# A decoder step on one core: late value pages also on ScalarE, key pages also on GpSimd, more slack for TensorE's small work, transfers issued by free buffer, and row scaling folded into a product

## The chip, the cores and the metric

One core of a Trainium2 chip. The time is the device time of one execution in microseconds, the median of several; the kernel before took 1545.37 us (three runs, 1544.26 to 1545.92). Engines are called PE (TensorE), DVE (VectorE), ACT (ScalarE), POOL (GpSimd) and SP (the queue that issues every DMA).

## The reference, cut to what matters

One layer of a hybrid decoder for 512 prompt tokens and 8 single-token samples, all in float32, model width 2048.

- Rows are normalised (`u = rms_norm(x, g_norm)`) and multiplied by `w_in` (2048 x 7168) into queries, keys, values, two gates and the input of a convolution. The prompt runs differential attention (two softmax maps per head, eight heads) and a 31-tap depthwise convolution with layer norm; both halves go through `w_out` (2048 x 2048), then `h += sigmoid(rmsnorm(h) W_pg) * (p W_ple)` and a last RMSNorm.
- The eight samples do the same for one token each, but attend to a paged cache of 4096 past keys and values: 8 x 32 pages of 128 positions, 512 KB per key page and per value page, found through `page_table`. For a sample, `score = q . k` for 16 maps per position, softmax over all positions, `a = p0 - lam * p1` per head, and `o[h] = sum over positions of a[pos, h] * v[pos, h, :]`.

So 256 key pages and 256 value pages (268 MB) are read beside some 70 MB of weights.

## The kernel before, in words

**Main products.** The weights come in slots of 256 x 512 (512 KB, tile `raw`, three buffers). Each half slot is split into a rounded part `hi` (ACT) and a rest `lo` (POOL, sometimes DVE), three buffers of each; the activations stand split as `aht` and `alt`. A half slot is 12 PE products into the four `acc` banks: hi x aht, hi x alt, lo x aht for four token tiles. The slots run in a fixed order: k, q, v, the convolution's inputs, the gates, `w_out`, `w_pw`, and in the end `w_ple` and `w_pg` with two half passes for the last columns.

**Everything else is small work laid between them.** The program is laid out at build time by a planner (class `Planner`, L61): it keeps an estimated clock for each engine (`clk`) and an estimated ready time for each tile (`plan.ready`). After every three main products `hook` (L354) runs: it issues weights and pages (`wpump`, `kring.pump`, `vring.pump`: SP), splits weights ahead, advances waiting tasks (generators with conditions made by `on`, L276), and calls `decode_tick` (L562). Each engine then runs its list in order, so a wrong estimate shows as a wait in the trace. PE's small work may only be placed at each fourth hook (`turn`, `TURNS`), that is after 12 main products, and `on("PE", ...)` asks that what it reads is ready 500 ns before PE's clock.

**Pages.** Key pages come through the ring `kt` (5 buffers), value pages through `vt` (2 buffers), and through `kt` too when no key is left to issue. A buffer is refilled when its reader is planned to end within 500 ns; the three sources are asked in a fixed order (weights, `kt`, `vt`). A key page is multiplied by the broadcast query `qb` on DVE (one 128x1024 TENSOR_TENSOR) and summed in groups of 64 by DVE (TENSOR_REDUCE) or, when DVE is planned over 400 ns late and no other such page is under way, by 16 ACT activations with an accumulator. When the 32 pages of a sample are summed, `softmax` makes `aw`. A value page is four PE products `pers<-vt,aw`, side by side in four column groups (two records each in the trace); `v_pages` (L607) takes all pages planned ready, one at the least at a group's last hook and two otherwise. `v_end` (L518) picks the heads out of `pers` when a sample's 32 pages are done. After the eighth, `sample_tail` (L1406) runs the samples through `w_out` and `w_pg` by "tail pages" through the same two rings.

**The start.** Four row tiles are loaded into `ct`, `dt` and two halves of `ft`. `rows_stat` makes the norm factor of each row, `rows_scale` (DVE) scales the first 512 columns, `rows_rest` (POOL, 12 calls) the other 1536, and PE transposes 128x128 blocks against the identity (`rows_T` for the first three column blocks, `u_T` for the other 13), four per block; `u_split` makes `aht` and `alt` from the transposed block. Two of the POOL calls stand before the fourth tile's statistics and ten stand after the second slot half's start, ahead of the `lo` splits that follow on POOL's list.

All instructions but a few are recorded under line 216 (the helper that emits them), so groups are told apart by tile names.

Of the kernel before, what the change touches and what calls it, by code (L numbers as in the profile page):

```python
# [221 lines left out]
def hymba_step(ctx, tc, x_prompt, x_sample, p_prompt, p_sample, cache_k, cache_v, state_conv, page_table,  # L222
# [123 lines left out]
    step = [0]  # L346

# [6 lines left out]
    def hook(n=7):  # L354
        step[0] = n
        wpump()
        kring.pump()
        vring.pump()
        if cur[0] < 168:
            split_ahead()  # L360
        for t in list(tasks):
            for _ in range(3):
# [33 lines left out]
    class Ring:  # L396
# [15 lines left out]
        def pump(self):  # L412
            while self.n < self.used + self.size and (self.n < self.size or self.freed[0] <= clk["PE"] + 500):
                kind = self.next_kind()
                if kind is None:
                    return
# [12 lines left out]
                self.n += 1  # L429

# [87 lines left out]
    def v_end(s):  # L518
# [7 lines left out]
        if vper[0] == s:  # L526
# [18 lines left out]
            yield from gather(ps)  # L545
        ended[0] += 1
# [6 lines left out]
    K_LATE = 400  # L553
# [8 lines left out]
    def decode_tick(at):  # L562
        if not dec["on"]:
            return
        now = clk["PE"]
        while True:
            more = k_next()
            pend = dec["pend"]
            if pend and (len(pend) > 1 or not more):
                s, pg, kt = pend[0]  # L570
                if k_act_live[0] < 1 and clk["A"] <= now + 300 and clk["V"] > now + K_LATE and plan.ready(kt) <= now + 800:
                    pend.pop(0)
                    k_act_live[0] += 1
                    spawn(k_act(s, pg, kt), rank=2)
                elif clk["V"] <= now + 400:
                    pend.pop(0)
                    V.tensor_reduce(out=dec["sc"][s][:, pg, :], in_=kt.rearrange("p (x d) -> p x d", d=64), axis=AX.X, op=ADD)
                    k_did(s, kt)
                else:
                    break  # L580
            elif more and clk["V"] <= now + 400:
                s, pg = divmod(dec["ik"], NPAGE)
                if pg == 0:
                    dec["sc"][s] = scp.tile([128, NPAGE, 16], F32, tag="sc", name="sc")
                kt, _ = kring.get()
                V.tensor_tensor(out=kt, in0=kt, in1=qbt[s], op=MUL)
                pend.append((s, pg, kt))
                dec["ik"] += 1
                if pg == NPAGE - 1 and s + 1 < NSEQ:
                    spawn(prep_qb(s + 1), rank=0)  # L590
            else:
                break
        v_pages(at == 7)

    def v_here():
# [9 lines left out]
        return n  # L605

# [1132 lines left out]
```

## Time and profile before

| | before |
|---|---|
| median of the runs | 1545.37 us |
| profiled execution | 1543.31 us, span 1541.5 us |
| PE busy | 1464.2 us, 95% of the span |
| DVE, ACT, POOL busy | 1089.7, 852.6, 627.3 us |
| DMA | 424.4 MB, mean 275 GB/s |

The span runs from the first to the last instruction; 1.8 us of the profiled execution lie outside it. PE's records overlap their neighbours (a product of 512 columns is recorded with some 0.4 us and the next begins 0.23 us later), so steps are read from starts and from the chain, not from the durations. A fp32 product leaves two records.

### The profile page before, as it was taken

The numbers are of one execution on the slowest core, as the hardware profiler recorded it, in microseconds if no ns is written. First come the engines' busy times: TensorE is split into PE (matmuls) and PEld (weight loads), VectorE is DVE, ScalarE is ACT, GpSimd is POOL, SyncE is SP. The second block draws the span as 40 slices with busy tenths as digits, with TensorE's granted clock in tenths as the row PEclk, the third lists the DMA queues.
The fourth block names the chain that finished last, engine by engine and source line by source line (L and its number), as shares of the span: only waits on it lengthen the run. The fifth ranks groups of instructions, "written<-read, shape, count | busy, mean of one in ns | idle before, by whom it ended". The sixth has DMA issues, their size and how long they took to land.

```text
span 1541.5 us, 32434 instructions
## 1 busy us (share of the span) xinstructions
PE 1464.2 (95%) x10448; PEld 1037.8 (67%) x10448; DVE 1089.7 (71%) x1625; ACT 852.6 (55%) x4162; POOL 627.3 (41%) x471
## 2 busy tenths in 40 slices
PE   5999999999999999999999999999999999999986
PEld 4677877766767666667767666677767776666653
DVE  5278888887998888888879789777787695110212
ACT  4256775666537566664456775656655675131332
POOL 5144534333433333333433445244333355343642
PEclk8999999999999999999999999999999999999998
DMA  8758779776877777674488848799887798999778
GB/s 292 270 175 289 268 259 372 275 283 232 283 260 236 256 264 247 219 247 151 153 307 281 301 155 296 259 355 349 304 325 261 252 379 315 351 328 346 268 265 283
DMA packets 148923, 424.42 MB, mean 275 GB/s; under 512 B 14192, under 2 KB 16226, under 8 KB 148480
## 3 DMA queue, kind: packets, MB, share of 16 engines
q1 hardware_dynamic: 148752, 422.35, 77.6%
q8 instruction: 82, 1.34, 0.4%
q14 instruction: 89, 0.73, 0.1%
HBM read 413.62 MB, written 9.63 MB: 275 GB/s over the span
## 4 chain that ended last, share of the span: by engine, by line
PE 73%; DMA 12%; DVE 6%; POOL 3%; ACT 2%; issue 2%; SPq 1%; POOLq 0%; ACTq 0%; DVEq 0%
PE acc L216 55%; PE pers L216 11%; PE misc L216 6%; DMA raw<-in_w_in_dram 4%; POOL lo L216 3%; DMA vt<-in_cache_v_dram 3%; DVE kt L216 2%; DMA raw<-in_w_out_dram 1%; DMA kt<-in_cache_k_dram 1%; DMA kt<-in_w_pg_dram 1%; SPq L216 1%; DVE sc L216 1%; ACT hi L216 1%; DVE bt L216 1%; DMA raw<-in_w_pg_dram 1%
## 5 line engine op out<-in xcount | busy, mean ns | idle before, releaser
L216 POOL TENSOR_TENSOR lo<-raw,hi 128x512 fp32r<-128x512 f32 x392 | 560.7, 1442 | 808.0 <-ACT hi L216 783.1
L216 ACT CAST hi<-raw 128x512 fp32r<-128x512 f32 x392 | 237.0, 617 | 431.4 <-PE acc L216 230.0
L216 ACT ACTIVATE kt<-kt 128x64 f32<-128x64 f32 x1568 | 378.5, 244 | 18.0 <-DVE kt L216 18.0
L216 PE MATMUL acc<-hi,aht 128*128 128x512 f32 x896 | 374.2, 418 | 7.8 <-ACT hi L216 7.6
L216 DVE TENSOR_TENSOR kt<-kt,qb 128x1024 f32<-128x1024 f32 x256 | 352.8, 1391 | 38.7 <-DMA kt<-in_cache_k_dram 35.3
L216 PE MATMUL acc<-lo,aht 128*128 128x512 f32 x896 | 359.9, 402 | 14.4 <-POOL lo L216 14.3
L216 PE MATMUL acc<-hi,alt 128*128 128x512 f32 x896 | 356.4, 398 | 0.2 <-DVE alt L216 0.2
L216 ACT ACTIVATION_READ_ACCUMULATOR kt<-kt 128x1 f32 x1568 | 296.3, 189 | 0.0
L216 PE MATMUL acc<-aht,hi 128*128 128x512 f32 x576 | 242.4, 421 | 4.2 <-ACT aht L216 3.4
L216 PE MATMUL acc<-aht,lo 128*128 128x512 f32 x576 | 229.6, 399 | 2.1 <-POOL lo L216 2.0
L216 PEld LDWEIGHTS acc<-hi,aht 128*128 128x128 f32 x896 | 169.7, 189 | 87.0 <-ACT hi L216 25.9
L216 PE MATMUL acc<-alt,hi 128*128 128x512 f32 x576 | 228.3, 396 | 0.0
L216 PEld LDWEIGHTS acc<-lo,aht 128*128 128x128 f32 x896 | 169.7, 189 | 65.8 <-POOL lo L216 26.1
L216 PEld LDWEIGHTS acc<-hi,alt 128*128 128x128 f32 x896 | 170.3, 190 | 34.4 <-DVE alt L216 0.8
L216 DVE TENSOR_REDUCE sc<-kt 128x16 f32<-128x1024 f32 x158 | 189.8, 1209 | 1.3
L216 DVE SCALAR_TENSOR_TENSOR misc<-ft,wdwT,misc 128x512 f32<-128x512 f32 x240 | 180.0, 750 | 6.3
L216 PEld LDWEIGHTS acc<-aht,hi 128*128 128x128 f32 x576 | 108.8, 189 | 64.3 <-issue 32.1
L216 PEld LDWEIGHTS acc<-aht,lo 128*128 128x128 f32 x576 | 108.7, 189 | 31.7 <-POOL lo L216 5.8
L216 PE MATMUL pers<-vt,aw 128*8 128x256 f32 x1656 | 114.1, 380 | 13.9 <-DVE pers L216 9.4
L216 PEld LDWEIGHTS acc<-alt,hi 128*128 128x128 f32 x576 | 108.9, 189 | 21.0 <-DVE alt L216 0.4
L216 DVE SCALAR_TENSOR_TENSOR acc<-acc,ct 128x512 f32<-128x512 f32 x16 | 11.2, 700 | 128.2 <-ACT acc L216 128.1
L216 PEld LDWEIGHTS pers<-vt,aw 128*8 128x8 f32 x1656 | 33.9, 88 | 67.5 <-issue 24.9
(259 smaller groups left out, 1273.2 us busy)
## 6 DMA issues: line engine op xcount, KB each, us to landing
kt<-in_cache_k_dram SPq DMA_DIRECT2D x256, 512.0 KB
vt<-in_cache_v_dram SPq DMA_DIRECT2D x207, 512.0 KB
raw<-in_w_in_dram SPq DMA_DIRECT2D x112, 512.0 KB
kt<-in_cache_v_dram SPq DMA_DIRECT2D x49, 512.0 KB
raw<-in_w_pg_dram SPq DMA_DIRECT2D x40, 512.0 KB
raw<-in_w_out_dram SPq DMA_DIRECT2D x32, 512.0 KB
kt<-in_w_in_dram SPq DMA_DIRECT2D x12, 512.0 KB
kt<-in_w_out_dram SPq DMA_DIRECT2D x12, 512.0 KB
```

Source lines behind the costliest of these rows:

```text
L216: real(*args, **kw)
```

## The change

1. `on("PE", ...)` asks for 800 ns of slack instead of 500; value pages taken by PE must be ready 600 ns before PE's clock instead of 0.
2. Weights, `kt` and `vt` are issued by one function `pump`, the buffer that comes free first first, and 300 ns ahead instead of 500.
3. Late value pages by ACT. When the last key page of the last sample has been multiplied, the buffer of `qb` becomes an accumulator (`vacc`). From then on a value page may go to ACT: eight activations of 128x128, each scaled by its head's weight in `aw`, in place (or straight into `vacc` for the first page), two pages at a time; DVE then adds the page to `vacc` (128x1024). While that is possible PE takes value pages only when four are ready. At the sample's end eight small PE products sum `vacc` over the positions.
4. Key pages: POOL may do the multiplication when DVE's clock is over 700 ns ahead of PE's and POOL's at least 100 ns behind; ACT may sum two pages at a time, already when DVE's clock is ahead of PE's at all (before 400 ns); any ready page may be taken, not only the oldest.
5. The rows are not scaled any more: a 128x128 diagonal `xg` per row tile (identity times the norm factor, DVE, one `tmp` buffer until the last block) is the right operand of a plain fp32 product in place of the transpose against the identity. The 12 POOL calls are gone, and the DVE calls shrink from 512 to 128 columns.

```diff
+    PE_BACK, V_BACK = 800.0, 600.0
...
-        back = -500.0 if eng == "PE" else 500.0
+        back = -PE_BACK if eng == "PE" else 500.0
...
-        wpump()
-        kring.pump()
-        vring.pump()
+        pump()
...
+    PUMP = 300
+    def pump():
+        while True:
+            due = [(d, n, f) for n, (d, f) in enumerate(((wdue(), lambda: wpump(once=True)), (kring.due(), lambda: kring.pump(True)),
+                                                          (vring.due(), lambda: vring.pump(True)))) if d is not None]
+            if not due or min(due)[0] > clk["PE"] + PUMP:
+                return
+            min(due)[2]()
...
+        if s in vacc:
+            ps = yield from take("misc")
+            V.memset(ps[:, 0:256], 0.0)
+            yield on("PE", ps[:, 0:256], vacc[s])
+            for h in range(8):
+                a, g = h // 4, h % 4
+                mm(ps[32 * g:32 * g + 8, a * 128:(a + 1) * 128], cst[:, C_ROW + 7 - s:C_ROW + 15 - s],
+                   vacc[s][:, h * 128:(h + 1) * 128], start=False, stop=True, cost=7 if g else 205)
+            va_free.append(plan.ready(vacc.pop(s), True))
+            yield from gather(ps)
...
-    K_LATE = 400
+    K_LATE, K_POOL, K_LIVE = 0, -100, 2
...
-                if k_act_live[0] < 1 and clk["A"] <= now + 300 and clk["V"] > now + K_LATE and plan.ready(kt) <= now + 800:
+                if k_act_live[0] < K_LIVE and clk["A"] <= now + 300 and clk["V"] > now + K_LATE:
...
+            eng = V if clk["V"] <= now + 400 else G if clk["G"] <= now + K_POOL and clk["V"] > now + 700 and len(pend) < 3 else None
...
+            eng.tensor_tensor(out=kt, in0=kt, in1=qbt[s], op=MUL)
...
+            elif pg == NPAGE - 1:
+                va_free.append(plan.ready(qbt[s], True))
+        v_aside()
         v_pages(at == 7)
...
+    V_ACT, V_LIVE = 300, 2
+    def v_aside():
+        now = clk["PE"]
+        while v_pend and clk["V"] <= now + 500 and v_pend[0][0] in va_has and plan.ready(v_pend[0][1]) <= now + 600:
+            s, vt, ring = v_pend.pop(0)
+            V.tensor_tensor(out=vacc[s], in0=vacc[s], in1=vt, op=ADD)
...
+            if clk["A"] > now + V_ACT or v_act_live[0] >= V_LIVE:
+                return
...
+    def v_act(s, pg, vt, ring, out, first):
+        for h in range(8):
+            c = slice(h * 128, (h + 1) * 128)
+            yield lambda: clk["A"] <= clk["PE"] + 400
+            A.activation(out=out[:, c], in_=vt[:, c], func=AF.Copy, scale=aw[s % 2][:, pg, h:h + 1])
...
-                if kind != VALS or idx // NPAGE != s or plan.ready(t) > clk["PE"]:
+                if kind != VALS or idx // NPAGE != s or plan.ready(t) > clk["PE"] - V_BACK:
...
+    V_MANY = 4
...
-        if n < (1 if tiled else 2) or not turn():
+        if n < (V_MANY if s_aside() else 1 if tiled else 2) or not turn():
...
-                PE.transpose(ps[:, t * 128:(t + 1) * 128], xt[t][k // 4][:, (k % 4) * 128:(k % 4 + 1) * 128], ident)
+                mm(ps[:, t * 128:(t + 1) * 128], xt[t][k // 4][:, (k % 4) * 128:(k % 4 + 1) * 128], xg[:, t * 128:(t + 1) * 128])
...
-            V.tensor_scalar(out=xbig[t][:, 0, :], in0=xbig[t][:, 0, :], scalar1=stat[:, 8 + t:9 + t], scalar2=None, op0=MUL)
+            V.tensor_scalar(out=xg[:, t * 128:(t + 1) * 128], in0=ident, scalar1=stat[:, 8 + t:9 + t], scalar2=None, op0=MUL)
...
-        def rows_rest(t, n):
-            x = xbig[t][:, n, :]
-            G.tensor_tensor(out=x, in0=x, in1=stat[:, 8 + t:9 + t].to_broadcast([128, 512]), op=MUL)
...
-        rows_rest(0, 1)
-        rows_rest(1, 1)
...
-                for n in range(1, 4):
-                    for t in range(2 if n == 1 else 0, 4):
-                        rows_rest(t, n)
```

## Rows read from the trace of the kernel before

**Rows 1.** The page, parts 1 and 2: busy time of each engine, and PE's and the DMA engines' busy share over 40 slices of the span, in tenths.

```profile
PE 1464.2 (95%) x10448; PEld 1037.8 (67%) x10448; DVE 1089.7 (71%) x1625; ACT 852.6 (55%) x4162; POOL 627.3 (41%) x471
PE   5999999999999999999999999999999999999986
...
DMA  8758779776877777674488848799887798999778
```

**Rows 2.** Busy time of each engine by stretch: the stretch and its length in us, then PE, weight loads, DVE, ACT, POOL (with counts), PE's granted clock, the DMA share and GB/s.

```profile
240.00:700.00 460.00, 448.55 (x3166) 313.16 (x3165) 395.31 (x731) 286.67 (x1435) 172.75 (x141) 1.00 0.75 261
700.00:960.00 260.00, 255.77 (x1759) 183.83 (x1759) 220.35 (x273) 152.91 (x816) 111.53 (x76) 1.00 0.69 236
...
1295.00:1427.00 132.00, 131.34 (x965) 84.65 (x965) 20.82 (x39) 31.91 (x76) 47.36 (x38) 1.00 0.96 346
1427.00:1541.50 114.50, 89.62 (x1024) 58.02 (x1022) 25.03 (x52) 37.87 (x77) 49.57 (x44) 0.96 0.77 272
```

**Rows 3.** What PE waited for over the whole span: us in total, times, longest.

```profile
PE acc L216 <- POOL lo L216: 16.6, 25, 4.9
PE pers L216 <- DVE pers L216: 10.1, 13, 2.8
...
PE misc L216 <- ACT tmp L216: 7.4, 5, 3.9
...
PE pers L216 <- DMA vt<-in_cache_v_dram: 4.4, 7, 1.5
```

**Rows 4.** The start: one group of POOL's row scaling (busy us, mean ns of one), then rows of the timeline (start us, us), then two stretches with the columns of rows 2.

```profile
L216 POOL TENSOR_TENSOR ft<-ft,stat 128x512 f32<-128x512 f32 x6 | 6.3, 1068 | 0.0
...
24.18 1.04 POOL L216 TENSOR_TENSOR ct<-ct,stat 128x512 f32<-128x512 f32 x1
...
32.16 2.48 POOL L216 TENSOR_TENSOR lo<-raw,hi 128x512 fp32r<-128x512 f32 x2
...
33.47 0.61 PE L216 MATMUL acc<-lo,aht 128*128 128x512 f32 x1 [4.86 <-POOL lo L216]
...
33.40:36.60 3.20, 3.13 (x14) 2.99 (x15) 0.80 (x2) 1.38 (x2) 2.47 (x3) 0.55 0.84 252
...
38.30:41.00 2.70, 2.70 (x21) 2.39 (x19) 1.41 (x2) 2.08 (x4) 0.11 (x1) 1.00 0.10 31
```

**Rows 5.** The chain of work that ended last (start us, us, what, records): the transposes of the start at two clock levels, six main products, visits to two and three value pages, the 12 main products between visits, and four fp32 products of 128x128x128 (two records each).

```profile
34.08 2.56 PE misc L216 x12
...
38.32 1.31 PE misc L216 x12
39.63 1.40 PE acc L216 x6
...
1295.92 0.98 PE pers L216 x16
1296.90 3.01 PE acc L216 x12
...
1304.89 1.41 PE pers L216 x24
...
1367.00 0.89 PE misc L216 x8
```

**Rows 6.** The instructions that read or write `aw` (PE's are the value pages, eight records a page), by stretch: PE, weight loads, DVE.

```profile
1295.00:1427.00 132.00, 34.95 (x544) 11.85 (x544) 0.43 (x1) 1.00 0.96 346
```

**Rows 7.** The instructions that read or write `qb` by stretch: DVE (the key multiplications, one a page) and ACT.

```profile
60.00:240.00 180.00, 69.99 (x50) 2.15 (x4) 1.00 0.76 269
240.00:700.00 460.00, 104.54 (x78) 2.15 (x4) 1.00 0.75 261
960.00:1295.00 335.00, 121.70 (x89) 2.15 (x4) 0.98 0.85 307
```

**Rows 8.** Groups of the whole span (busy us, mean ns of one, idle before): the key multiplication and its sum on DVE, the sum by ACT, ACT's scaled copy of 128x128, and POOL's split.

```profile
L216 DVE TENSOR_TENSOR kt<-kt,qb 128x1024 f32<-128x1024 f32 x256 | 352.8, 1391 | 38.7 <-DMA kt<-in_cache_k_dram 35.3 <-ACT qb L216 2.6
L216 DVE TENSOR_REDUCE sc<-kt 128x16 f32<-128x1024 f32 x158 | 189.8, 1209 | 1.3
L216 ACT ACTIVATE kt<-kt 128x64 f32<-128x64 f32 x1568 | 378.5, 244 | 18.0 <-DVE kt L216 18.0
L216 ACT ACTIVATE bt<-misc,vec 128x128 f32<-128x128 f32 x32 | 11.4, 364 | 5.5 <-PE misc L216 5.3
L216 POOL TENSOR_TENSOR lo<-raw,hi 128x512 fp32r<-128x512 f32 x392 | 560.7, 1442 | 808.0 <-ACT hi L216 783.1 <-PE acc L216 12.4 <-PE misc L216 6.1
```

**Rows 9.** Timeline of POOL and DVE from 1270 to 1294 us (start us, us).

```profile
1289.38 1.28 POOL L216 TENSOR_TENSOR bt<-bt,tmp 128x512 f32<-128x512 f32 x1
1290.62 2.27 POOL L216 TENSOR_TENSOR lo<-raw,hi 128x512 fp32r<-128x512 f32 x1
...
1271.98 1.21 DVE L216 TENSOR_TENSOR kt<-kt,qb 128x1024 f32<-128x1024 f32 x1
...
1290.42 3.55 DVE L216 TENSOR_TENSOR kt<-kt,qb 128x1024 f32<-128x1024 f32 x2
```

**Rows 10.** One of PE's waits from 1440 us to the end (us in total, times, longest), and the last piece of the chain in which PE works (start us, us).

```profile
PE misc L216 <- DMA kt<-in_w_pg_dram: 2.8, 5, 0.9
...
1524.10 0.91 PE acc L216 x3
```

More of the change, by code (lines that the diff above doesn't have):

```diff
@@ L361, in hook @@
         for t in list(tasks):
-            for _ in range(3):
+            for _ in range(STEPS):
                 if t[0] is not None and not t[0]():
@@ L410, in next_kind, with due, pump @@
             return TAIL if left[TAIL] else None
-        def pump(self):
-            while self.n < self.used + self.size and (self.n < self.size or self.freed[0] <= clk["PE"] + 500):
+        def due(self):
+            if self.n >= self.used + self.size or self.next_kind() is None:
+                return None
+            return self.freed[0] if self.n >= self.size else 0.0
+        def pump(self, once=False):
+            while self.due() is not None and self.due() <= clk["PE"] + PUMP:
                 kind = self.next_kind()
-                if kind is None:
-                    return
                 idx = issued[kind]
@@ new lines, in decode_tick @@
+            pend.append((s, pg, kt))
+            dec["ik"] += 1
+            if pg == NPAGE - 1 and s + 1 < NSEQ:
+                spawn(prep_qb(s + 1), rank=0)
+            elif pg == NPAGE - 1:
+                va_free.append(plan.ready(qbt[s], True))
+        v_aside()
+        v_pages(at == 7)
+    va_free, vacc, va_has, v_act_live, v_pend = [], {}, set(), [0], []
+    V_ACT, V_LIVE = 300, 2
[4 more added lines that the diff above has]
+            V.tensor_tensor(out=vacc[s], in0=vacc[s], in1=vt, op=ADD)
+            ring.done(vt)
+            v_did(s)
+        while True:
+            ring = v_ring(600)
+            s, pg = divmod(dec["iv"], NPAGE)
+            if ring is None or not dec["soft"][s] or plan.ready(aw[s % 2]) > now + 500 or not (s in vacc or va_free) or len(v_pend) > 2:
+                return
+            if clk["A"] > now + V_ACT or v_act_live[0] >= V_LIVE:
+                return
+            first = s not in vacc
+            if first:
+                vacc[s] = plan.begin(qbp.tile([128, 1024], F32, tag="qb", name="qb"), va_free.pop(0))
+            vt, _ = ring.get()
+            dec["iv"] += 1
+            out = vacc[s] if first else vt
+            v_act_live[0] += 1
+            spawn(v_act(s, pg, vt, ring, out, first), rank=2)
@@ L595, in v_here, with v_did, v_ring @@
+    def v_did(s):
+        vdone[s] += 1
+        if vdone[s] == NPAGE:
+            spawn(v_end(s), rank=0)
+    def v_ring(ahead=0):
+        best = min((r for r in (kring, vring) if r.tiles and r.tiles[0][1] == VALS), key=lambda r: r.tiles[0][2], default=None)
+        return best if best and best.tiles[0][2] == dec["iv"] and plan.ready(best.tiles[0][0]) <= clk["PE"] + ahead else None
     def v_here():
@@ L614, in v_pages @@
         for k in range(n):
-            ring = kring if kring.here(VALS) and (not vring.here(VALS) or kring.tiles[0][2] < vring.tiles[0][2]) else vring
+            ring = v_ring(-V_BACK)
+            if ring is None:
+                break
             vt, idx = ring.get()
@@ L749, in hymba_step, with wdue, wpump @@
     raw_freed = []
-    def wpump(most=RAWB):
-        while (wst["issued"] < len(slots) and wst["issued"] < wst["released"] + most
-               and (wst["issued"] < RAWB or raw_freed[0] <= clk["PE"] + 500)):
+    def wdue():
+        if wst["issued"] >= min(len(slots), wst["released"] + RAWB):
+            return None
+        return raw_freed[0] if wst["issued"] >= RAWB else 0.0
+    def wpump(most=RAWB, once=False):
+        while wdue() is not None and wst["issued"] < wst["released"] + most and wdue() <= clk["PE"] + PUMP:
             at = raw_freed.pop(0) if wst["issued"] >= RAWB else 0
@@ L759, in wpump @@
             wst["issued"] += 1
+            if once:
+                return
     def release(i):
```

57 lines of the change are left out of this document (34 added, 23 removed).

## Prediction, on record before the result

> **What bounds the kernel now.** I read the page's shares first [rows 1]: PE is busy 95% of the span and at nine tenths or more in 37 of the 40 slices, the DMA engines mostly between six and nine tenths. So PE's list bounds, and a microsecond counts only if it leaves that list or a gap in it. Next, busy time by stretch [rows 2]. From 240 to 960 us PE is full, DVE is at 86% (395.3 of 460 us) and then 85%, POOL at 38% and 43%. From 1295 us, after the last key page, PE is busy 131.3 of 132 us, DVE only 20.8, ACT 31.9, while the DMA engines stand at 0.96 and 346 GB/s. From 1427 us, after the last value page, PE falls to 89.6 of 114.5 us. Then PE's waits [rows 3]: 16.6 us for `lo`, 10.1 for a memset of `pers`, 7.4 for a tile of ACT, 4.4 for value pages. They are small because the layout leaves slack.
>
> The sum is made against the profiled execution: 1543.31 us, of which the span is 1541.5 and 1.81 us lie around it. The median of the runs, 1545.37, is 2.06 us above it; I carry the change of the span over to the median.
>
> **Part by part. A: the start.** Twelve row scalings leave POOL. One of `ft` takes 1.07 us, they stand ahead of the `lo` split that begins at 32.16 us, and PE waits 4.86 us for that split [rows 4]. With POOL free the split can follow its `hi` at once, so I let the whole 4.86 us go. PE then runs slowly for a while: twelve transposes take 2.56 us at 34 us and 1.31 us at 38 us [rows 5], with a granted clock of 0.55 and 1.00 [rows 4], near the lower (1.2 GHz) and at the higher (2.4 GHz) of its two levels, the lower one after those 4.86 us of idle time; this 1.25 us goes too, with nothing taken for the main products between. Against it, 52 transposes (13 blocks of four) become plain fp32 products. A transpose takes 1.31/12 = 0.11 us, four fp32 products of the same size 0.89 us, so 0.22 us each [rows 5]: 52 x 0.11 = 5.7 us on PE's list. The first 12 stand where PE waits for rows anyway, and DVE's scaling before them shrinks to a quarter of its columns: nothing. Sum -4.9 - 1.3 + 5.7 = -0.5 us; ends -6.2 (if the products fit into waits for ACT's and DVE's splitting of the blocks) and +5.7 (if another input is late where `lo` was).
>
> **B: late value pages.** 544 records in the stretch from 1295 us are 68 pages [rows 6]. A visit to two or three pages lasts 0.98 or 1.41 us [rows 5]: 0.43 us a page and 0.12 beside. The 12 main products between visits take 3.01 us, against 2 x 1.40 = 2.80 for two times six that follow other main work [rows 5], so a visit costs 0.12 + 0.21 = 0.33 us beyond its pages. ACT's scaled copy of 128x128 takes 364 ns [rows 8], eight of them 2.9 us. ACT is idle 132 - 31.9 = 100 us of this stretch [rows 2], enough for 34 pages, half of them. The Trainium skill ("ScalarE: Activation LUTs", on the cost of an activation) gives 186 ns + 0.833 ns a column, 93 more for a pointer operand, and an overlap of 93 between neighbours; eight would take 2.3 us and 43 pages fit, an estimate. I keep the row, which has no back-to-back copies to show an overlap. 34 pages x 0.43 = 14.6 us leave PE. Visits: at 2 to 3 pages the 68 pages make some 30 visits now; the other 34 pages, taken four at a time, make nine, so 21 x 0.33 = 6.9 us more. Back come two ends of samples, each two rows of four products side by side and a visit: 2 x (0.44 + 0.33) = 1.5 us. Sum -20 us. DVE's sum of 34 pages, 1.39 us each by the multiplication's row [rows 8], is 47 us beside 20.8 busy ones: hidden. If all 68 went, it would be -29.2 - 9.9 + 1.5 = -38; if the DMA engines set this stretch, it could be 0 (second rival).
>
> **C: slack.** Of PE's waits [rows 3], more slack can reach those for value pages (4.4 us) and for ACT's tiles (7.4, of which the longest, 3.9, I leave standing). 4.4 + 3.5 = 7.9 at best; I take -6 us. The 10.1 us on `pers` stays: no readiness test looks at that memset. The price is that each step of a chain (attention, softmax) may miss its place and come one turn later, 3.0 us. Main work follows it on PE, so it costs nothing until the layout has to stand still for a chain; lower end 0, upper -8, and +4 if a few turns are lost where PE has nothing else.
>
> **D: key pages.** While DVE is loaded with the convolution and attention, 78 keys are multiplied in 460 us; before that, 50 in 180 us [rows 7]. POOL and a second ACT page lift the slow rate; if it came up to the fast one, 460 x 50/180 = 128 keys would fit, 50 more. I take a quarter, 13 keys, at the late rate of 89 in 335 us [rows 7] some 49 us of earlier end. PE does not wait for keys, so this by itself is worth nothing. Its worth is at the end: value pages, and with them the samples' last chain, move forward under main work. After 1427 us PE is idle 24.9 us [rows 2]; from its last product at 1525 us [rows 10] 16.5 us are stores and the last norm and stay, 8.4 can be filled. I take -5 us, ends 0 and -8.4; the loss is the third rival.
>
> **E: issue order.** An order by free buffer keeps SP from standing before a full buffer while another is free; 300 ns ahead instead of 500 takes up to 0.2 us of lead from each transfer. PE waits 4.4 us for value pages [rows 3] and 2.8 for `w_pg` pages at the end [rows 10]. I take 0; ends -3 and +3. SP's list holds the stores too; none is on the chain before the end.
>
> Sum: -0.5 - 20 - 6 - 5 + 0 = -31.5 us. Span 1510.0, profiled execution 1511.8, median 1545.4 - 31.5 = **1513.9 us**.
>
> **The rivals.** *First, more comes off* (chance 0.14). The earlier end of the keys leaves more value pages to ACT, nearly all 68 go (-38), the idle 8.4 us at the end fill, and waits shrink by 8: -0.5 - 38 - 8.4 - 8 = -55, 1490 us. For it: ACT is 76% idle there [rows 2]. Against: a page under ACT keeps its buffer some 3 to 6 us, and seven buffers fill up, upon which PE finds its four.
>
> *Second, the DMA engines set the end* (0.15). From 1295 to 1427 us they are busy at 0.96 [rows 2]. Freed PE time then only brings main products forward, and their weights use the same engines. If B's 20 us are lost but for the part that the stretch after 1427 us (0.77, 272 GB/s) absorbs, say a quarter, the sum is -0.5 - 5 - 6 = -11.5: 1534 us. Against: that last stretch moves 114.5 x 0.272 = 31 MB, which at 346 GB/s would take 90 us, so 24 us of room are there. That ACT gets hardly a page, since its accumulator is free only after the last key, ends in the same place.
>
> *Third, key pages on POOL make `lo` late, slower than before* (0.14). POOL's two-input pass over 512 columns takes 1.28 us alone, and 2.27 us beside DVE's key multiplications, two of which then take 3.55 us instead of 2 x 1.21 [rows 9]. A key page is 1024 columns: 2.6 us alone, 4.5 beside such DVE work. A half slot lasts 3.0 us on PE, three are kept split, and POOL finishes `lo` about two ahead, 6 us less 0.6 for `hi` and 1.3 to 2.3 for `lo`: some 3 us of slack. A key of 4.5 us overruns it by 1.5 us. With 50 such keys PE would wait 75 us: -31.5 + 75 = +43, 1589 us at the far end; with 30, +13, 1559 us. It decides from 21 keys (21 x 1.5 = 31.5). For it: `lo` is PE's longest wait already [rows 3]. Against: only DVE operations with two inputs in SBUF collide in these rows, the convolution's taps read PSUM, and the layout begins a key on POOL only when POOL is idle. The Trainium skill speaks for this rival: "SBUF — State Buffer", on who interferes with whom, says that such a DVE operation and a reading GpSimd operation share one port pair as an exclusive lock, and "GPSIMD Engine Reference" advises against GpSimd for elementwise work; rows 9 agree with the lock.
>
> **How the numbers follow.** Forecast 0.57, its own range 1498 to 1530 us (B between 10 and 30, D and C at their ends). First rival 0.14, second 0.15, third 0.14. What a measurement can tell from no change is about 0.2%, 3 us. Faster by more: 0.57 + 0.14 + 0.12 of the second = 0.83. Within 0.2%: 0.03 of the second and 0.02 of the third, 0.05. Slower: 0.12. The range of 8 in 10 reaches 1482 (most of the first rival) to 1543 us (the second); outside are the third rival and the extreme of the first.
>
> **What would show it.** A: no `lo` wait above 2 us before 50 us, and two records per block in the start. B: ACT's 128x128 copies of `vt` and `kt` near 34 pages (270 instructions), PE's records on `aw` after the last key halved, PE still busy over 97% there. C: the wait for `vt` below 2 us. D: the last key multiplication near 1245 us, 10 to 40 of them on POOL, PE's wait for `lo` below 25 us. E: no change in SP's waits that PE sees. The prediction is wrong if PE's busy time falls by less than 10 us, if the wait for `lo` grows past 40 us, or if PE gets gaps in the value stretch with the DMA engines at 0.96 or more.

## The result, and the profile after

The changed kernel takes **1561.49 us** (median of five runs, 1555.1 to 1565.9) against 1545.37 before: 1.1% slower, ratio 1.0113 [1.0075, 1.0152]. Forecast were 1513.9 us, with a chance of 0.83 for faster. The profiled execution took 1565.28 us with a span of 1563.5.

The page, parts 1 and 2, of the kernel after (as [rows 1]):

```profile
PE 1466.3 (94%) x10280; PEld 1051.2 (67%) x10280; DVE 1049.7 (67%) x1522; ACT 1032.2 (66%) x5274; POOL 880.8 (56%) x574
PE   7998999999998999999998999889999999989994
...
DMA  8757889888785976786696978878988679958553
```

PE is busy as long as before, and its line has eights at slices 4, 13, 22, 26, 27 and 36, where it had nines. The stretches of [rows 2], after:

```profile
240.00:700.00 460.00, 444.48 (x3136) 310.86 (x3135) 388.15 (x663) 326.19 (x1813) 295.52 (x189) 1.00 0.80 278
700.00:960.00 260.00, 249.99 (x1776) 177.54 (x1775) 218.40 (x293) 185.85 (x1099) 176.47 (x105) 0.98 0.74 258
...
1295.00:1427.00 132.00, 127.72 (x948) 94.28 (x946) 45.46 (x61) 75.74 (x203) 59.24 (x46) 1.00 0.79 276
```

In the 460 us from 240 to 700 us POOL went from 172.75 to 295.52 us, while DVE shed only 7 us. The groups say why (as [rows 8]; busy us, mean ns of one, idle before):

```profile
L216 DVE TENSOR_TENSOR kt<-kt,qb 128x1024 f32<-128x1024 f32 x141 | 207.2, 1483 | 39.5 <-DMA kt<-in_cache_k_dram 34.8 <-ACT kt L216 2.9 <-ACT qb L216 1.7
L216 DVE SCALAR_TENSOR_TENSOR misc<-ft,wdwT,misc 128x512 f32<-128x512 f32 x240 | 180.1, 751 | 6.3
L216 DVE TENSOR_REDUCE sc<-kt 128x16 f32<-128x1024 f32 x132 | 158.1, 1212 | 14.5 <-POOL kt L216 13.2
...
L216 DVE TENSOR_SCALAR o<-o,oq 128x128 f32<-128x128 f32 x32 | 20.5, 641 | 8.1 <-POOL oq L216 8.1
...
L216 DVE TENSOR_TENSOR rt<-tmp,cst 128x128 f32<-128x128 f32 x32 | 18.6, 621 | 0.8 <-ACT tmp L216 0.6
...
L216 DVE TENSOR_SCALAR ft<-ft,vec 128x512 f32<-128x512 f32 x8 | 12.7, 1582 | 0.3
...
L216 POOL TENSOR_TENSOR kt<-kt,qb 128x1024 f32<-128x1024 f32 x115 | 290.6, 2533 | 57.6 <-DMA kt<-in_cache_k_dram 32.0 <-ACT qb L216 14.8 <-ACT kt L216 5.5
```

POOL multiplied **115** key pages, 2.53 us each; the forecast had reckoned with 10 to 40. The same three groups of small DVE work in the kernel before:

```profile
L216 DVE TENSOR_TENSOR rt<-tmp,cst 128x128 f32<-128x128 f32 x32 | 12.0, 416 | 4.9 <-ACT tmp L216 4.8
...
L216 DVE TENSOR_SCALAR o<-o,oq 128x128 f32<-128x128 f32 x32 | 9.6, 300 | 6.1 <-POOL oq L216 5.9
...
L216 DVE TENSOR_SCALAR ft<-ft,vec 128x512 f32<-128x512 f32 x8 | 6.0, 754 | 0.3
```

The scalings doubled (300 to 641, 754 to 1582 ns) and `rt` rose from 416 to 621 ns, while the convolution's taps, which read PSUM, stayed at 751 and the sums by TENSOR_REDUCE at 1212. Not all of the rise is the keys' doing: without any key on POOL (e1 below) the three means are 441, 995 and 302 ns, since POOL's `lo` splits collide with some of these instructions too. The busy times are small; what matters is that these groups are links of chains that PE waits for. PE's waits after (as [rows 3]):

```profile
PE acc L216 <- POOL lo L216: 15.2, 28, 1.3
PE pers L216 <- DVE pers L216: 14.1, 12, 4.1
PE misc L216 <- DVE tmp L216: 14.0, 6, 8.4
PE pers L216 <- DMA vt<-in_cache_v_dram: 13.1, 8, 3.2
PE acc L216 <- ACT hi L216: 12.5, 9, 2.6
```

The wait for `lo` did not grow. The waits for value pages tripled (4.4 before). Their loads are issued by SP in order, behind key loads that wait for a key buffer. One of SP's waits grew: between 150 and 1080 us the DMA queue waited for DVE's sums

```profile
SPq L216 <- DVE sc L216: 79.2, 38, 7.4
```

against 47.5 us in the kernel before. That this made the value pages late is not shown: SP's longest wait there, for PE's products on `pers`, which free the value buffers, fell from 229.9 to 208.1 us, and e13 below keeps the late value pages without POOL's reads. Of the 14.0 us for `tmp`, 8.4 are one wait at the start, where the kernel before waited 8.6 us for a load. Where PE stands still longest behind the start, DVE has chained layer-norm work and POOL a run of keys. The timeline there (start us, us), DVE, then POOL, then PE:

```profile
1010.70 2.46 DVE L216 TENSOR_SCALAR ft<-ft,vec 128x512 f32<-128x512 f32 x1
1013.08 3.37 DVE L216 TENSOR_TENSOR kt<-kt,qb 128x1024 f32<-128x1024 f32 x1
1016.37 2.84 DVE L216 SCALAR_TENSOR_TENSOR ft<-tmp,ft 128x512 f32<-128x512 f32 x1
...
1019.84 2.46 DVE L216 TENSOR_SCALAR ft<-ft,vec 128x512 f32<-128x512 f32 x1
...
1010.08 8.58 POOL L216 TENSOR_TENSOR kt<-kt,qb 128x1024 f32<-128x1024 f32 x3
...
1020.60 1.04 PE L216 MATMUL pers<-vt,aw 128*8 128x256 f32 x8 [2.59 <-DMA vt<-in_cache_v_dram]
1024.01 0.80 PE L216 MATMUL acc<-aht,hi 128*128 128x512 f32 x1 [2.36 <-ACT aht L216]
```

Beside three keys of POOL each of these DVE instructions lasts about as long as one of POOL's: 2.46 us for a scaling that takes 0.55 us in the kernel before when no split of POOL runs beside it. DVE and POOL take turns here, an instruction each, and the chain of work that ended last runs through the layer norm's `ft` on DVE. PE has only late value pages to do until 1024 us.

Where the 16 us went is best seen in the main products, PE's instructions on `acc`, by stretch (us of the stretch, PE busy and count). Before:

```profile
15.00:1295.00 1280.00, 992.93 (x3909) 0.99 0.76 268
1295.00:1427.00 132.00, 97.62 (x384) 1.00 0.96 346
```

After:

```profile
15.00:1295.00 1280.00, 951.06 (x3729) 0.98 0.80 280
1295.00:1427.00 132.00, 108.04 (x436) 1.00 0.79 276
```

By 1295 us the changed kernel is 180 products behind, at 0.25 us each (12 in 3.01 [rows 5]) 45 us, of which 6.5 are value pages done earlier: the last key is multiplied at 1162.5 us instead of 1291.7, and PE has done 203 value pages by 1295 us against 188, 0.43 us each [rows 5]. Then it gains 52 products in 132 us, since ACT takes value pages: 13 us there.

### The profile page after: what moved, and what is told of

It is laid out like the page before. It is cut to its first block, busy times and chain, and to the rows that moved or that the text cites. A ratio compares the mean times of both kernels' runs of the same rounds, so it can differ in the third digit from the quotient of the medians.

```text
span 1563.5 us, 33329 instructions
## 1 busy us (share of the span) xinstructions
PE 1466.3 (94%) x10280; PEld 1051.2 (67%) x10280; DVE 1049.7 (67%) x1522; ACT 1032.2 (66%) x5274; POOL 880.8 (56%) x574
## 4 chain that ended last, share of the span: by engine, by line
PE 70%; DMA 10%; DVE 9%; ACT 4%; issue 3%; POOL 3%; SPq 0%; POOLq 0%; ACTq 0%; DVEq 0%
PE acc L216 54%; PE pers L216 9%; PE misc L216 8%; DMA raw<-in_w_in_dram 3%; POOL lo L216 3%; DVE misc L216 2%; DMA raw<-in_w_out_dram 1%; ACT kt L216 1%; DMA raw<-in_w_pg_dram 1%; DVE ft L216 1%; DVE kt L216 1%; ACT hi L216 1%; DVE bt L216 1%; DMA vt<-in_cache_v_dram 1%; DVE tmp L216 1%
## 5 line engine op out<-in xcount | busy, mean ns | idle before, releaser
L216 POOL TENSOR_TENSOR lo<-raw,hi 128x512 fp32r<-128x512 f32 x392 | 544.8, 1402 | 554.7 <-ACT hi L216 522.7
L216 ACT ACTIVATE kt<-kt 128x64 f32<-128x64 f32 x1984 | 477.9, 244 | 25.7 <-DVE kt L216 20.0
L216 PE MATMUL acc<-hi,aht 128*128 128x512 f32 x896 | 374.0, 417 | 11.9 <-ACT hi L216 11.4
L216 ACT ACTIVATION_READ_ACCUMULATOR kt<-kt 128x1 f32 x1984 | 374.9, 189 | 0.0
L216 POOL TENSOR_TENSOR kt<-kt,qb 128x1024 f32<-128x1024 f32 x115 | 290.6, 2533 | 57.6 <-DMA kt<-in_cache_k_dram 32.0
L216 DVE TENSOR_TENSOR kt<-kt,qb 128x1024 f32<-128x1024 f32 x141 | 207.2, 1483 | 39.5 <-DMA kt<-in_cache_k_dram 34.8
L216 DVE TENSOR_REDUCE sc<-kt 128x16 f32<-128x1024 f32 x132 | 158.1, 1212 | 14.5 <-POOL kt L216 13.2
L216 PE MATMUL pers<-vt,aw 128*8 128x256 f32 x1480 | 105.6, 391 | 25.8 <-DMA vt<-in_cache_v_dram 13.1
```

The costliest lines, as they stand in the source:

```text
L216: real(*args, **kw)
```

## The experiments

Two theories stand at first. **P**: POOL's keys cost the time. **Others**: ACT's early and doubled key sums (theory A), or the larger slack (S).

**e1, no keys on POOL.**

```diff
-    K_LATE, K_POOL, K_LIVE = 0, -100, 2
+    K_LATE, K_POOL, K_LIVE = 0, -1e9, 2
```

> The changed kernel, but POOL never multiplies a key page (all 256 on DVE; ACT still sums up to two pages at a time). Theory P (POOL's 115 key pages hold up DVE operations with two inputs in SBUF, the chains behind DVE run late and PE stands): the middle of the kernel, in which the changed one fell 50 us behind, keeps at least 30 us of that, so 1515 to 1530 us, and DVE's 128x128 scaling of o falls back from 641 to about 300 ns. Theory A (ACT's extra key sums are what makes things late): no gain, 1555 to 1570 us. Theory S (the larger slack for PE's small work delays the chains): no gain either.

**1538.5 us**, ratio to before 0.9951 [0.9923, 0.9979]. 23 us came back, of the 30 or more that theory P expected. The scaling of `o` fell too, but not to 300 ns:

```profile
L216 DVE TENSOR_SCALAR o<-o,oq 128x128 f32<-128x128 f32 x32 | 14.1, 441 | 7.6 <-POOL oq L216 7.6
```

Read one by one, 23 of the 32 have nothing of POOL beside them and take 0.25 to 0.29 us; the eight beside a `lo` split take 0.27 to 1.39.

**e2, the key handling of before** inside the changed kernel.

```diff
-    K_LATE, K_POOL, K_LIVE = 0, -100, 2
+    K_LATE, K_POOL, K_LIVE = 400, -1000000000.0, 1
...
-            x = next((x for x in pend if plan.ready(x[2]) <= now + 700), None)
+            x = pend[0] if pend else None
...
-                if k_act_live[0] < K_LIVE and clk["A"] <= now + 300 and clk["V"] > now + K_LATE:
+                if k_act_live[0] < K_LIVE and clk["A"] <= now + 300 and clk["V"] > now + K_LATE and plan.ready(kt) <= now + 800:
```

> The changed kernel with the old handling of key pages: DVE multiplies all, ACT sums one page at a time and only when DVE is planned 400 ns late. Theory P: as without POOL's keys, 1510 to 1530 us; the difference to that kernel is what ACT's second page does. Theory A: only this one gains, to 1515 to 1530 us. Theory S: 1550 us or more.

1547.61 us, 1.0003 [0.9976, 1.0030]. No theory's range held it, and theory A, by which only this kernel gains, is out. ACT's earlier and doubled sums, with the choice of any ready page, are no loss; they are what separates e1 from this, 9 us in e1's favour.

**e3, POOL's keys**, put into the kernel before. The free choice of a ready page for the sum comes with them.

```diff
+            eng = V if clk["V"] <= now + 400 else G if clk["G"] <= now + K_POOL and clk["V"] > now + 700 and len(pend) < 3 else None
...
+            eng.tensor_tensor(out=kt, in0=kt, in1=qbt[s], op=MUL)
```

> The kernel before with POOL's key multiplications alone (ACT's share as before, no late pages on ACT, old slack, issue order and row scaling). Theory P: it loses the middle and has no late gain, so slower than the kernel before by 20 to 50 us, 1565 to 1595 us. Theories A and S: within 10 us of the kernel before, or faster through earlier keys.

**1608.78 us**, 1.0364 [1.0288, 1.0439]. POOL took 136 keys of 2492 ns, and the 128x128 scaling of `o` rose from 300 to 1134 ns. P holds: some +62 us without the rest of the change, above the 20 to 50 expected, and removing it pays.

**e4, the old slack.**

```diff
-    PE_BACK, V_BACK = 800.0, 600.0
+    PE_BACK, V_BACK = 500.0, 0.0
```

> The changed kernel with the old slack (500 ns for PE's small work, none for value pages). Theory S: 1515 to 1535 us, since chains take fewer turns and PE does not stand 14 us before the convolution's products near 1010 us. Theories P and A: 1555 to 1570 us, with PE's waits for value pages back at 4 us or more.

1564.0 us, 1.0121 [1.0055, 1.0186]: beside POOL's keys the slack makes no difference that these runs can tell.

**What of POOL's keys costs: reading or being occupied?** e6 and e7 are e1 with extra POOL work at some 90 places, in one and the same order of instructions.

```diff
+                    for _ in range(6):
+                        G.tensor_tensor(out=gsB, in0=cst[:, 0:128], in1=cst[:, 392:520], op=MUL, cost=390)
```

> The changed kernel without key pages on POOL; at some 80 places where POOL would have taken one, six POOL multiplications of two SBUF inputs, 128x128 into an unused tile, stand instead. Nobody reads what they write. Theory P1 (POOL's reading of SBUF stretches VectorE's instructions, and their chains feed PE late): slower than the kernel without POOL's keys (1538) by 15 us or more, VectorE's 128x128 and 128x512 instructions lengthened as in the changed kernel (300 ns to 500 or more). Rival P2 (POOL is occupied, so its own lo and additions come late): this kernel and the next one, with fills in the same places, lose alike.

e7 puts two fills (`memset` of `gsB`) in the place of each multiplication.

> The same kernel with two fills of 128x128 (no SBUF input) at the place of each of those multiplications: POOL about as long occupied, but reading nothing. Theory P1: within 5 us of the kernel without POOL's keys (1538), VectorE's instructions as short as there. Rival P2 (occupied POOL): as slow as the run with the multiplications.

1629.65 us, 1.0524 [1.0460, 1.0589], and 1617.54 us, 1.0461 [1.0399, 1.0523]. Both are far above e1. By what was expected, the pair speaks for P2: e7 missed P1's number by 79 us, and the two lose nearly alike, with overlapping intervals. But it is a poor test: the planner laid keys later, so the last value page begins at 1531.2 and 1515.7 us instead of 1410.9, and the span ends 97 and 96 us behind it, about the least of all runs (table below). Between the two lie 12 us, but POOL's multiplications were also longer (625 ns against two fills of 206). e13 does it better.

**e13, fills in place of POOL's keys**, every instruction else in the changed kernel's order.

```diff
-            eng.tensor_tensor(out=kt, in0=kt, in1=qbt[s], op=MUL)
+            if eng is G:
+                plan.put("G", "tensor_tensor", (), dict(out=kt, in0=kt, in1=qbt[s], op=MUL))
+                G.real.memset(kt, 0.0)
+                G.real.memset(kt, 0.0)
+                G.real.memset(kt[:, 0:512], 0.0)
+            else:
+                V.tensor_tensor(out=kt, in0=kt, in1=qbt[s], op=MUL)
```

> The changed kernel with all instructions in its order, but POOL fills each of its key pages (two fills of 128x1024 and one of 128x512) in place of multiplying it: some 2.5 us of POOL each as before, and no SBUF input read. This leaves out the multiplication of those key pages. Theory P1 (POOL's two-input reading stretches VectorE's instructions): VectorE's 128x128 scaling of o falls from 641 ns to under 350, the waits for pers and vt to a few us, the time to 1535 to 1545 us. Rival P2 (POOL occupied, buffers free late): 1555 to 1565 us, as the changed kernel.

**1540.29 us**, 0.9958 [0.9932, 0.9984]. Its groups:

```profile
L216 DVE TENSOR_SCALAR o<-o,oq 128x128 f32<-128x128 f32 x32 | 14.8, 464 | 10.1 <-POOL oq L216 9.7 <-POOL kt L623 0.3
...
L216 DVE TENSOR_TENSOR rt<-tmp,cst 128x128 f32<-128x128 f32 x32 | 10.3, 363 | 3.1 <-ACT tmp L216 2.9
...
L622 POOL MEMSET kt<- 128x1024 f32 x115 | 110.2, 958 | 38.9 <-DMA kt<-in_cache_k_dram 37.3 <-DVE kt L216 1.6
```

POOL is occupied 958 + 956 + 527 = 2441 ns a page, nearly as long as by a key, in the same order; without the reading 21 us are gone. By 1295 us the profiled execution (1549.72 us) has done 63 more main products than the changed kernel's (3792 against 3729), 16 us, which is what separates the two (1565.28 us). So the loss is P1, POOL's reads against DVE's. Two of my numbers missed. The two-input `rt` is back at 363 ns, but the one-input scaling only at 464, not under 350. The 350 was set too low, for e1 has 441 without key or fill; the means do not tell whether fills stretch the scaling. Single instructions do:

```profile
310.86 0.95 POOL L622 MEMSET kt<- 128x1024 f32 x1
310.95 0.94 DVE L216 TENSOR_SCALAR o<-o,oq 128x128 f32<-128x128 f32 x1 [0.66 <-POOL oq L216]
```

Of nine scalings beside fills alone eight take 0.60 to 0.95 us, against 0.28 to 0.29 with nothing of POOL beside them; all 15 `rt` beside fills alone take 0.28 to 0.29, where those with nothing of POOL beside them take 0.27 to 0.29. The Trainium skill ("SBUF — State Buffer", on who interferes with whom) says that a TENSOR_SCALAR in a two-port mode contends with GpSimd too, while two-input operations contend only with a GpSimd operation that reads SBUF; these instructions agree. And the waits for `pers` (11.9 us) and for value pages (11.9) stay, against 3.9 and 0.3 in e1: they come with POOL as a third engine for keys, not from the port; that the order in which value pages, keys and loads are laid does it is argued, not shown.

**e8, keys on POOL only from the products `w_pw` on.**

```diff
-            eng = V if clk["V"] <= now + 400 else G if clk["G"] <= now + K_POOL and clk["V"] > now + 700 and len(pend) < 3 else None
+            eng = V if clk["V"] <= now + 400 else G if cur[0] >= 120 and clk["G"] <= now + K_POOL and clk["V"] > now + 700 and len(pend) < 3 else None
```

> The changed kernel with keys on POOL only from the pw products on (after the standing layer norm, some 40 of the 115). Theory P1 with E: the stretch before the pw products is as without POOL's keys, the keys and so the samples' end come earlier, and few VectorE chains stand after the layer norm: 1520 to 1537 us, faster than 1538. Rival (each key on POOL costs the same wherever it stands, some 0.2 us): 1543 to 1550 us.

1537.33 us, 0.9945 [0.9916, 0.9974], with 15 keys on POOL (some 40 expected), just outside the theory's range and the same as e1. These 15 cost nothing measurable and gained nothing.

**Why is e1 at 1538 and not near 1514?** After 1295 us e1 holds the forecast gain: 442 main products by 1427 us against 384. Then it idles. The stretches before and behind its last value page (columns of [rows 2]):

```profile
1295.00:1411.00 116.00, 112.89 (x661) 82.91 (x659) 46.50 (x47) 88.60 (x252) 59.90 (x44) 1.00 0.82 297
1411.00:1532.70 121.70, 80.88 (x958) 53.55 (x958) 23.50 (x51) 28.62 (x57) 37.24 (x33) 0.81 0.72 250
```

In the last 122 us PE is busy 81: after 1427 us it has 129 main products left (before: 222), too few to cover the samples' own chain (`v_end`, `w_out`, `w_pg`). Theory **E**: two paths end the kernel, the main products and the samples' path behind the last value page, and the later one decides. Rival **B**: PE's busy time decides, as forecast.

**e5, only the late value pages**, in the kernel before.

```diff
+            elif pg == NPAGE - 1:
+                va_free.append(plan.ready(qbt[s], True))
+        v_aside()
```

> The kernel before with the late value pages on ACT and nothing else of the change (no keys on POOL, old slack, old order of loads, old scaling of the rows). The late pages shift the work as forecast (some 30 value pages leave PE, so the main products run some 20 us ahead after the last key). Theory E (the end is set by the samples' own path from their last value page, so what PE saves earlier is idle time at the end): 1540 to 1548 us, with the lead of the main products gone in the last stretch. Rival B (PE's busy time sets the time, as forecast): 1522 to 1530 us.

1543.27 us, 0.9983 [0.9953, 1.0014]: worth nothing alone. The last value page begins at 1450.9 us, before at 1424.8.

**e9, visits from two waiting pages on**, in e1.

```diff
-    V_MANY = 4
+    V_MANY = 2
```

> The changed kernel without POOL's keys, and PE takes the value pages of a sequence from two waiting pages on instead of four, so PE does more of them and the last value page is done sooner. Theory E (the end is set by the samples' path from their last value page): the last value page some 15 us sooner than 1410, the time 1525 to 1533 us, below the 1538 of the kernel without POOL's keys, although PE is busy longer. Rival B (PE's busy time sets the end): 1542 to 1550 us, some 10 us above it.

**1520.58 us**, 0.9878 [0.9840, 0.9917]. That is below the range expected of E, and far below B's. The last value page begins at 1394.6 instead of 1410.9 us, and the end follows. PE was to take more pages; ACT takes more (31 against 28). PE's busy time falls by 5.5 us (1456.1 to 1450.6), the time by 18, so the busy time does not explain it. The stretches as for e1:

```profile
1295.00:1395.00 100.00, 98.83 (x567) 73.45 (x566) 49.53 (x48) 87.96 (x257) 47.99 (x36) 1.00 0.93 335
1395.00:1514.00 119.00, 88.54 (x1026) 58.99 (x1024) 27.76 (x52) 35.07 (x71) 48.92 (x42) 0.89 0.72 253
```

The chain of waits of e9 shows what the samples' path is made of (start us, us): pieces of `w_out` and `w_pg`, through the page rings (`kt`, `vt`) for the samples and through `raw` for the main products.

```profile
1422.95 6.27 DMA kt<-in_w_out_dram
...
1436.87 8.05 DMA vt<-in_w_pg_dram
1445.00 9.81 DMA raw<-in_w_pg_dram
...
1485.83 8.56 DMA vt<-in_w_pg_dram
```

**e10, the same in e8.**

> The kernel with POOL's keys from the pw products on, with the same visits from two waiting pages on. Theory E: 1520 to 1530 us, below both its parent (1537) and the kernel without POOL's keys. Rival B: 1541 to 1550 us.

1526.72 us, 0.9906 [0.9885, 0.9926]: faster than e8 as E says, but not ahead of e9.

**e11, e1 without the late value pages** (the line that hands `qb` to `va_free`, shown at e5, is out; PE's visits are then as in the kernel before, from two pages on or from one at a group's last hook).

> The changed kernel without POOL's keys and without the late value pages on ACT. Theory E: as no PE page is saved and none is late, 1535 to 1545 us, within 5 us of the kernel with the late pages (1538): the late pages are worth nothing. Rival B (late pages are worth the 20 us forecast): 1552 to 1562 us.

1539.76 us, 0.9972 [0.9954, 0.9991], as E says. With e9 beside it: late pages, visits from two pages on, are worth 1539.8 - 1520.6 = 19 us; with visits from four on (e1) nothing.

**e14, visits from two pages on in the changed kernel, POOL's keys included.**

> The changed kernel, POOL's keys included, with visits from two waiting value pages on. There the value pages ended near 1370 us and the main products were the later path, so by theory E (the later of the two paths decides) more PE work for value pages gains nothing: 1558 to 1570 us. Rival (visits from four pages on are bad in themselves, by some 18 us): 1540 to 1547 us.

1565.96 us, 1.0123 [1.0083, 1.0164]: no gain, as E says, for in the changed kernel the last value page begins at 1370.5 us, 193 us before the end, with 348 main products left after 1427 us: they are the later path. The constant is not bad in itself.

**e16, visits from one page on**, in e1 (`V_MANY = 1`).

> No keys on POOL, visits from one waiting page on. Theory E with two paths near balance: PE takes more pages and more visits, ACT fewer, the value pages end a little sooner: 1518 to 1527 us, no better than with two. Rival (the samples' path still decides alone): 1508 to 1516 us.

1530.67 us, 0.9912 [0.9885, 0.9939]: outside the range given for E and worse than two. The last value page begins at 1386.4 us, sooner than in e9, and the main products are only some 19 behind e9's at 1427 us (118 left against 99), 5 us. What grew is PE's wait, behind the last value page, for the samples' `w_out` pages:

```profile
PE misc L216 <- DMA kt<-in_w_out_dram: 10.5, 7, 2.9
```

That and 2.5 us in the other ring stand against 2.3 us in e9. So the end may hang on a third thing, when the samples' own weights are loaded; why they come later here stays open.

All spans against the last value page (start of its last instruction on PE, ACT or DVE, and what follows):

| kernel | last value page | span | between |
|---|---|---|---|
| e6, e7 | 1531.2, 1515.7 | 1628.5, 1612.1 | 97, 96 |
| e5, e2 | 1450.9, 1449.2 | 1548.0, 1548.6 | 97, 99 |
| e8, e17 | 1423.1, 1435.8 | 1530.3, 1543.1 | 107, 107 |
| e18, e15, e12 | 1422.5, 1401.1, 1414.3 | 1533.9, 1514.4, 1529.5 | 111, 113, 115 |
| before | 1424.8 | 1541.5 | 117 |
| e9, e1, e10 | 1394.6, 1410.9, 1395.5 | 1514.1, 1532.7, 1519.7 | 119, 122, 124 |
| e16 | 1386.4 | 1527.4 | 141 |
| e11 | 1383.5 | 1535.1 | 152 |
| after, e13 | 1370.5, 1351.3 | 1563.5, 1547.1 | 193, 196 |
| e4, e14, e3 | 1362.2, 1360.0, 1363.8 | 1558.8, 1573.8, 1609.4 | 197, 214, 246 |

No kernel ends less than 96 us behind its last value page. Up to 124 us I take the samples' path to decide, from 152 on the main products; e16 is neither. This is a sorting, not a measurement, and within the first group the ends still differ by 28 us. Runs that were made to test E against a rival are e5, e9, e10, e11 and e14; they went its way.

**e12, the old order of the loads**, in e1 (`wpump()`, `kring.pump()`, `vring.pump()`, 500 ns).

> The changed kernel without POOL's keys, loads issued in the old order (weight pieces first, then key buffers, then value buffers). Theory D2 (at the end the weight pieces w_pg queue behind the samples' weights, 10.4 us for one piece at 1405 us, because the new order gives the key ring its turn by free time): 1525 to 1533 us, that wait gone. Rival: the order is worth nothing, 1535 to 1541 us; the same bytes pass and only who waits changes.

1533.95 us, 0.9947 [0.9928, 0.9965]: between the two ranges, but the kernel before was also 4 us faster in this set (1543.03), and the ratio is e1's. The order is worth nothing there.

**e15, e9 with the old order of the loads.**

> No keys on POOL, visits from two pages on, and loads in the old order. The order of the loads was worth nothing with four pages: 1516 to 1524 us, as the kernel with the new order (1520.6). Rival (with the samples' path shorter, the weight pieces w_pg decide the end, and the old order, which issues them first, gains): 1505 to 1514 us.

**1517.31 us**, 0.9820 [0.9782, 0.9859], the fastest; inside the range of the first theory. Its interval meets e9's, so the order cannot be told from nothing here either.

**e17, the kernel before with late value pages and visits from two on** (e5 with `V_MANY = 2`).

> The kernel before with the late value pages on ACT, and PE's visits from two waiting pages on instead of four; nothing else. If the late pages are worth their forecast and only the wait for four pages lost it: 1522 to 1530 us against the 1543 with four. Rival (they need the new start and slack beside them to gain): 1537 to 1545 us.

1544.81 us, 0.9986 [0.9961, 1.0011]: the rival. Late pages alone gain nothing, and value pages end no sooner than before (1435.8 us).

**e18, e15 with the old slack** (the diff of e4).

> No keys on POOL, visits from two pages on, old order of loads, and the old slack of 500 and 0 ns. If the slack is worth what was forecast: 1521 to 1526 us, 4 to 8 above the same kernel with the new slack (1517). Rival (slack worth nothing, as beside POOL's keys): 1514 to 1520 us.

**1536.44 us**, 0.9949 [0.9926, 0.9972]: 19 us above e15, more than I had given the slack at all. PE's waits of e18:

```profile
PE pers L216 <- DVE pers L216: 15.2, 14, 5.4
...
PE pers L216 <- DMA vt<-in_cache_v_dram: 5.9, 10, 1.2
```

and of e15:

```profile
PE pers L216 <- DVE pers L216: 8.6, 11, 2.9
...
PE pers L216 <- DMA vt<-in_cache_v_dram: 2.5, 4, 1.5
```

10 us of waits are gone with the slack, also at `pers`, which the forecast had left out. e15 has done 57 more main products by 1295 us (3933 against 3876, 14 us), and its last key is multiplied at 1244.5 instead of 1275.6 us, so both paths gain.

## Why the prediction was wrong, point by point

**The step that failed is D, in its count and in the path of its cost.** The sum took D at -5 us, with "10 to 40 of them on POOL": POOL took 115, because the layout gives it a key each time that DVE's clock is 700 ns ahead and POOL's 100 behind, and this came true 115 times. The loss was priced in the third rival alone, which had the sign and the cause (POOL's two-input reads against DVE's), at a chance of 0.14. Its place was wrong: it let `lo` be late, and the `lo` wait stayed at 15.2 us. What came late were DVE's own small operations and the chains behind them; with fills in place of the reads 21 us are gone (e13). That its 1559 us at 30 keys lies near the 1561 measured with 115 is luck. Its price of 1.5 us a key was too high: e1 against after gives 23 us for 115 keys, 0.2 us each. The keys without the rest cost some 62 us (e3, 136 keys), so the price depends on what else gives room. The prediction weighed a collision by the engine that starts it; the engine that is held up was the busier one, at 86%. Its remark that only two-input operations collide holds for the rows it read, and is too narrow for the trace: in the kernel before, two of the eight layer-norm scalings, with one input, took 1.37 and 1.39 us beside a `lo` split and the other six 0.55. Of its own signs of being wrong one came: PE's busy time did not fall (1464.2 to 1466.3 us).

**B's size was right, and its condition was missing.** 35 pages went to ACT (34 forecast), and PE gained main products in the stretch where that was forecast. A copy takes 0.39 us in place, and seven in a row 2.16, so eight some 2.45, where my row gave 2.9; and ACT was busy 75.7 of the 132 us, so its room was not what limited the count. The prediction's estimate from the Trainium skill ("ScalarE: Activation LUTs", "What ACT_TABLE_LOAD costs") was 2.3 us, nearer to what this trace shows. The surcharge of a visit was read against six products that stand behind transposes, not behind main work [rows 5]; the step is the same in long runs of main products (60 in 14.23 us in e9), so the number stands. But "taken four at a time, make nine, so 21 x 0.33 = 6.9 us more" counted as a gain what becomes the loss once POOL's keys are gone: waiting for four pages holds up the value pages, and the samples' path behind them ends the kernel. There, with two pages the late pages bring 19 us (e9 against e11), close to the -20 forecast; with four nothing (e1 against e11); alone in the kernel before nothing with either (e5, e17). In the changed kernel itself B's gain shows as the 52 products in the stretch after 1295 us, and only reduces the loss.

**C was undersized, and hidden.** -6 us were forecast; 19 were measured in the best kernel (e18 against e15), none beside POOL's keys (e4). That "the 10.1 us on `pers` stays" was wrong.

**A** went as said in the one place that was read: PE's `lo` wait before 60 us fell from 5.8 to 1.0 us. The hundredth main product begins at 68.5 us in both kernels, so the start gained next to nothing, as its sum of -0.5 has it; it was not tried alone. **E** at 0 holds (e12), in e15 perhaps a little better with the old order.

**D without POOL** is worth 9 us (e1 against e2), where -5 was forecast; the last key is multiplied at 1252.2 instead of 1284.0 us, and the last value page begins 38 us sooner.

**The second rival** (DMA engines) had the wrong stretch: the DMA share from 1295 to 1427 us fell to 0.79, and PE did gain there. That pieces of 4 to 10 us stand in e9's chain behind the last value page is its grain of truth.

Without POOL's keys and the wait for four pages, and with the old order of loads, the same change gives 1517 us, -28 against a forecast of -31.5. That the sums are so near is in part luck: C brought three times its term, and B's and C's gains need each other, so the terms do not add up as forecast. What stays open: how much of the loss behind e13 (its middle is still 117 products, 29 us, behind before, partly early pages) is the order of work and how much later loads; e13 and e1 come to the same time by different paths.

## What to carry to other kernels

Before work is given to an idle engine, look at which operations of the busier engine it collides with and who waits for those: the cost shows as longer means of small groups in another engine's chain, not as a wait on the engine that got the work. Where two paths end near each other, price every term on both; a batching rule that saves time on one can hold up the other, and two changes can need each other: without POOL's keys, the new slack without late pages gives 0.3% (e11), late pages with the old slack 0.5% (e18), both together 1.2 and 1.8% (e9, e15); a kernel with neither was not run. Count how often a condition in a layout comes true before you price it.

## What the runs showed of the hardware

A one-input DVE scaling of 128x512 that takes 0.55 us with no split of POOL beside it took 2.46 us between POOL's two-input multiplications of 128x1024 (2.4 to 3.5 us each), and DVE's TENSOR_REDUCE (1212 ns against 1209) and PSUM-reading taps (751 against 750) none longer. Fills by POOL left two-input DVE operations of 128x128 alone (15 of 15 at most 0.29 us) and stretched eight of nine one-input scalings to 0.60 to 0.95 us, from 0.28 to 0.29, where a fill takes 0.96 (e13).

Of PE's granted clock, e1 shows a fall: PE waited 5.88 us for `hi` before 1416.45 us, and from 1414 to 1420.8 us the granted clock was 0.50, the lower of its two levels (1.2 and 2.4 GHz); products of 512 columns then began 0.43 us apart, and 0.23 us apart once it was back at 1.00. Over the last 122 us of e1, in which it changed between the levels, it was 0.81 in the mean, over the last 114 of the kernel before 0.96 [rows 2].
